# A two-layer trunk: first products of three feed-forwards by seven block products in place of eight

## The chip, the cores and the metric

The kernel runs on one core of a Trainium2 chip. The metric is the device time of one execution in microseconds (us); a median over several executions is given, and the profile shows one execution instruction by instruction. The engines are named as in the profile: PE (TensorE, matrix products; PEld is its loading of weights), DVE (VectorE), ACT (ScalarE), POOL (GpSimd), SP (issues the loads).

## The reference, cut to what matters

```python
def ffn_sublayer(x, mod, k, g, w_in, w_out):
    h = modulated_norm(x, mod, k, g)              # RMS norm, (1 + scale), shift
    gt, up = jnp.split(h @ w_in, 2, axis=-1)      # 1024 -> 2 x 2816
    return x + 0.5 * mod[:, None, 3 * k + 2] * ((jax.nn.silu(gt) * up) @ w_out)
...
def ada_params(cond, w_ada, b_ada):               # shifts, scales and gates of a layer
    m = jax.nn.silu(cond) @ w_ada + b_ada         # 1024 -> 9 x 1024, for two conditions
...
# two layers, each: feed-forward, mixer (attention, pooling, convolution), feed-forward
# 128 context tokens and 512 latent tokens, all float32, 1024 channels
```

## The kernel before

There are six stages, one for each sublayer (l, n): feed-forwards (0,0), (0,2), (1,0) and (1,2), and a mixer (n = 1) in each layer. In the trace they lie at about 20 to 531 us, (0,0); 531 to 779, mixer; 779 to 1268, (0,2); 1268 to 1753, (1,0); 1753 to 1991, mixer; 1991 to 2466, (1,2).

The 640 tokens stay on the chip, channels on the partitions (`xT`, eight tiles of 128 channels), and are worked on in two halves of 320 columns. A float32 product is made of three in a reduced float32 format (`mm3`): weights and inputs are each split into a high and a low part, and high·high, high·low and low·high are summed in PSUM. `split_w` does that for a weight tile: ACT copies the high part (L163), POOL subtracts to give the low part (L164). For an input DVE subtracts (`split`, L149 and L150).

A feed-forward has 22 tiles j of 128 gate columns and 128 up columns. For each tile `up(j)` loads a gate and an up weight tile (128 x 1024, one load of 512 KB each), and multiplies each with the eight channel tiles of both halves: 2 x 2 x 8 x 3 = 96 matmuls of 128x128 by 320 columns. `gated` then takes the SiLU of the gate (ACT, L476), multiplies with up (DVE, L477) and splits the result into `g`. After certain tiles `down(ch)` multiplies a group of finished tiles (`FF_CHUNKS`, here of 6, 6, 6 and 4 tiles) with the second weights and adds the result to the tokens (`update_x`, L407); the last group goes through `last_product`, beside the norm of the next stage.

The modulation (`ada_params`) of later sublayers is computed beside the feed-forwards, in 32 chunks of 512 columns: 14 in (0,0), 11 in (0,2), 7 in (1,0), none in (1,2). A chunk (`ada_vector`) has four loads of 512 KB into `adaw` and, on DVE, two multiplications by a column (L287) and 14 multiply-adds (L289), all of 128x512, into a tile `part`. Later `side` ends it: eight small products on PE sum `part` over its partitions ("the pick", L296), DVE copies the sums (L252), PE transposes them (L253), DVE adds the bias (L254). `spread` says after which tiles a chunk is ended and the next one begun.

Loads, tiles and semaphores are handed out by a framework that also orders each engine's instructions. A tile of a pool with n buffers can be written only when the one handed out n tiles before it has been read for the last time. The pools that matter: `raw` (3 buffers, weights as loaded), `adaw` (2), `wh` and `wl` (4 each, split weights), `part` (1 buffer), `acc` (4 PSUM banks).

## Time and profile before

| | before |
|---|---|
| median of 3 runs (lowest to highest) | 2467.27 us (2467.14 to 2467.51) |
| span of the profiled execution | 2466.6 us |
| PE busy | 2387.6 us, 97% of the span, 16414 matmuls |
| DVE busy | 1346.8 us, 55% |
| ACT busy | 747.1 us, 30% |
| POOL busy | 786.3 us, 32% |
| loads into SBUF and stores | 246.58 MB, 100 GB/s over the span |

The profiled execution's own time is its span, 2466.6 us; it stands 0.7 us below the median of the runs. Shares are means over stages that differ: a feed-forward keeps PE busy nearly throughout, a mixer less. DVE's share differs between feed-forwards by the number of modulation chunks in them.

### The profile page before, as it was taken

How to read it: one execution, taken by the hardware profiler on the slowest of the kernel's cores; microseconds unless marked ns; L12 is line 12 of the kernel's file. 1: busy time of each engine (PE TensorE's matmuls, PEld its weight loads, DVE VectorE, ACT ScalarE, POOL GpSimd, SP SyncE). 2: the span in 40 equal slices, each digit the busy share in tenths (PEclk: the TensorE clock that was granted, in tenths of full speed). 3: DMA queues.
4: the chain of work that ended last, by engine and by line, in shares of the span. 5: the costliest groups of instructions: out<-in, count | busy, mean ns of one | idle time of the engine just before them, and what ended most of it. 6: DMA issues, size and time to landing. Idle time of an engine off the chain costs nothing.

```text
span 2466.6 us, 39767 instructions
## 1 busy us (share of the span) xinstructions
PE 2387.6 (97%) x16414; PEld 2311.5 (94%) x16414; DVE 1346.8 (55%) x2550; ACT 747.1 (30%) x1405; POOL 786.3 (32%) x383
## 2 busy tenths in 40 slices
PE   7999999999898999999999999999998989999999
PEld 6999999989878999999989999999897789999999
DVE  5565747877867464536683435253787662222222
ACT  4322222244455222222142222221454642221221
POOL 2433333333311433233323333333332133333331
PEclk9999999999999999999999999999999999999999
DMA  8444545523201443434423324232221022223221
GB/s 277 119 138 137 162 128 162 175 60 80 53 27 35 118 139 112 137 112 137 146 60 108 107 86 129 78 117 81 68 64 43 18 77 67 80 69 86 77 61 69
DMA packets 357246, 246.58 MB, mean 100 GB/s; under 512 B 25704, under 2 KB 317896, under 8 KB 357064
## 3 DMA queue, kind: packets, MB, share of 16 engines
q1 hardware_dynamic: 356884, 243.97, 33.3%
q8 instruction: 129, 2.11, 0.4%
q14 instruction: 53, 0.43, 0.1%
q10 hardware_dynamic: 180, 0.07, 0.0%
HBM read 241.12 MB, written 2.88 MB: 99 GB/s over the span
## 4 chain that ended last, share of the span: by engine, by line
PE 82%; DVE 12%; issue 2%; DMA 2%; ACT 2%; POOL 0%; ACTq 0%; DVEq 0%; SPq 0%; POOLq 0%
PE acc L329 26%; PE acc L330 25%; PE acc L331 25%; DVE part L289 3%; DVE tmp L378 1%; PE po L930 1%; DMA adaw<-in_w_ada 1%; PE acc L890 1%; PE mis L941 1%; DVE ssq L240 1%; DVE g L150 1%; DVE qw L762 1%; DVE x L407 1%; DVE t L341 1%; DVE h L394 1%
## 5 line engine op out<-in xcount | busy, mean ns | idle before, releaser
L164 POOL TENSOR_TENSOR wl<-raw,wh 128x1024 fp32r<-128x1024 f32 (+1 forms) x330 | 757.5, 2296 | 1568.5 <-ACT wh L163 1472.2
L329 PE MATMUL acc<-h,wh 128*128 128x320 f32 (+1 forms) x3264 | 1022.4, 314 | 14.9 <-ACT h L393 9.2
L330 PE MATMUL acc<-h,wh 128*128 128x320 f32 (+1 forms) x3264 | 1019.6, 313 | 14.0 <-DVE h L394 10.1
L331 PE MATMUL acc<-h,wl 128*128 128x320 f32 (+1 forms) x3264 | 1013.5, 311 | 0.0
L329 PEld LDWEIGHTS acc<-h,wh 128*128 128x128 f32 x3264 | 619.3, 190 | 25.5 <-ACT h L393 11.2
L330 PEld LDWEIGHTS acc<-h,wh 128*128 128x128 f32 x3264 | 619.7, 190 | 19.1 <-DVE h L394 12.5
L163 ACT ACTIVATE wh<-raw 128x1024 fp32r<-128x1024 f32 (+1 forms) x332 | 330.7, 996 | 1008.1 <-PE acc L330 507.7
L331 PEld LDWEIGHTS acc<-h,wl 128*128 128x128 f32 x3264 | 620.6, 190 | 0.2 <-issue 0.2
L330 PE MATMUL acc<-g,wh 128*128 128x320 f32 x1408 | 437.0, 310 | 0.0
L329 PE MATMUL acc<-g,wh 128*128 128x320 f32 x1408 | 435.9, 310 | 0.0
L331 PE MATMUL acc<-g,wl 128*128 128x320 f32 x1408 | 434.6, 309 | 0.0
L289 DVE SCALAR_TENSOR_TENSOR part<-adaw,c,part 128x512 f32<-128x512 f32 x448 | 363.0, 871 | 28.6 <-DMA adaw<-in_w_ada 28.6
L477 DVE TENSOR_TENSOR sg<-acc,sg 128x320 f32<-128x320 f32 x132 | 61.1, 488 | 498.8 <-PE acc L331 496.9
L407 DVE SCALAR_TENSOR_TENSOR x<-acc,gate,x 128x128 f32<-128x128 f32 (+2 forms) x384 | 155.4, 434 | 305.7 <-PE acc L331 305.4
L329 PEld LDWEIGHTS acc<-g,wh 128*128 128x128 f32 x1408 | 264.4, 188 | 1.6 <-issue 1.4
L331 PEld LDWEIGHTS acc<-g,wl 128*128 128x128 f32 x1408 | 265.3, 188 | 0.2
L330 PEld LDWEIGHTS acc<-g,wh 128*128 128x128 f32 x1408 | 264.3, 188 | 0.3
L150 DVE TENSOR_TENSOR g<-sg,g 128x320 fp32r<-128x320 f32 x176 | 187.4, 1100 | 31.6 <-ACT g L149 29.8
L476 ACT ACTIVATE sg<-acc 128x320 f32<-128x320 f32 x132 | 56.9, 431 | 300.6 <-PE acc L331 289.8
L329 PE MATMUL acc<-mix,wh 128*128 128x320 f32 x256 | 83.2, 325 | 13.2 <-DVE u L856 12.7
L149 ACT ACTIVATE g<-sg 128x320 fp32r<-128x320 f32 x176 | 75.5, 462 | 45.1 <-DVE sg L477 25.9
L331 PE MATMUL acc<-mix,wl 128*128 128x320 f32 x256 | 82.5, 322 | 0.0
(170 smaller groups left out, 1591.9 us busy)
## 6 DMA issues: line engine op xcount, KB each, us to landing
raw<-in_w_ffn_in SPq DMA_DIRECT2D x176, 512.0 KB
adaw<-in_w_ada SPq DMA_DIRECT2D x144, 512.0 KB
raw<-in_w_ffn_out SPq DMA_DIRECT2D x96, 384.0 KB
raw<-in_w_in SPq DMA_DIRECT2D x20, 512.0 KB
raw<-in_w_ffn_out SPq DMA_DIRECT2D x16, 512.0 KB
raw<-in_w_in SPq DMA_DIRECT2D x16, 256.0 KB
raw<-in_w_out SPq DMA_DIRECT2D x8, 512.0 KB
raw<-in_w_out SPq DMA_DIRECT2D x16, 256.0 KB
```

The source lines that it names most:

```text
L149: nc.scalar.activation(h, src, AF.Copy)
L150: nc.vector.tensor_tensor(lo, src, f32(h), op=ALU.subtract)
L163: nc.scalar.activation(h, raw, AF.Copy)
L164: eng.tensor_tensor(lo, raw, f32(h), op=ALU.subtract)
L240: nc.vector.tensor_tensor(ssq[:, c:e], ssq[:, c:e], sq[:, : e - c], op=ALU.add)
L289: nc.vector.scalar_tensor_tensor(part[:, j, :], r[:, k, :], c, part[:, j, :], op0=ALU.mult, op1=ALU.add)
L329: nc.tensor.matmul(out, wh, xh, start=start, stop=False)
L330: nc.tensor.matmul(out, wh, xl, start=False, stop=False)
L331: return nc.tensor.matmul(out, wl, xh, start=False, stop=stop)
L407: nc.vector.scalar_tensor_tensor(xT[t][:, s:e], ps[:, s - a : e - a], gates[l][n][:, t, j : j + 1], xT[t][:, s:e], op0=ALU.mult, op1=ALU.add,)
L476: nc.scalar.activation(sg, gate[:, :HALF], AF.Silu)
L477: nc.vector.tensor_tensor(sg, up[:, :HALF], sg, op=ALU.mult)
```

## The change: what it does

In the feed-forwards (0,2), (1,0) and (1,2) the tiles j = 3 to 21 are computed by seven block products in place of eight: 19 tiles in each, 57 in all. (0,0) and tiles 0 to 2 stay as they are. A block is half of the channels (four channel tiles) by half of the tokens, for up or for gate. Plainly a tile needs 2 x 2 x 2 = 8 such products of 4 x 3 = 12 matmuls; now there are seven, 84 matmuls, over sums of weight blocks and of input blocks.

- The input sums are made once in a stage (`seven`).
- The weight sums are made for each tile (`fast_weights`): four additions of 128x512 on DVE give two tiles of sums, `one` and `two`, in a new pool `sums` of two buffers. The low parts of both are made on DVE (128x1024 each), those of the up tile (128x1024) and of a quarter of the gate tile (`late`, 128x512) on POOL. ACT makes three high parts of 128x1024 and one of 128x512, in place of two of 128x1024.
- The results are put together from PSUM: ACT copies three of 128x320 out (`kept`), DVE adds three to them (`added`). Products 3 and 4 and the gating of tile j (`fast_ends`) come after product 1 of tile j + 1; `a` and `c` are `acc` banks, `b` is a bank of the mixer's pool `one_p`.

To make room: `raw` (now 4 buffers) serves weights and modulation loads alike, `part` of a modulation chunk is now one of the two `sums` tiles, several small tiles share nine `tmp` buffers, and the mixers load their tables each time. `FF_CHUNKS` has five groups (5, 5, 4, 4, 4), those of four with two column tiles to a load.

The comments were taken out of the file, so line numbers differ.

```diff
-FF_CHUNKS = ((0, 6), (6, 12), (12, 18), (18, 22))
+FF_CHUNKS = ((0, 5), (5, 10), (10, 14), (14, 18), (18, 22))
+PLAIN = 3
...
-    rawp = pool("raw", 3)
-    adaw = pool("adaw", 2)
+    rawp = pool("raw", 4)
...
+    sump = pool("sums", 2)
...
     def split_w(raw, nk, width, eng=nc.gpsimd):
...
-        part = small.tile([P, 2, 512], F32, name="part", bufs=1)
+        part = sum_tile().rearrange("p (j c) -> p j c", j=2)
         for q in range(4):
-            r = load_ada(l, ci, q, adaw.tile([P, 2, 512], F32, tag="adaw", name="adaw"))
+            r = load_ada(l, ci, q, raw_tile().rearrange("p (k c) -> p k c", k=2))
...
+        def fast_weights(j):
+            nk = KD // 2
+            up, *_ = load_raw(w_in, DFF + j * P)
+            gate, *_ = load_raw(w_in, j * P)
+            a1, a2, d1, d2 = up[:, :nk, :], up[:, nk:, :], gate[:, :nk, :], gate[:, nk:, :]
...
+            one, two = view(sum_tile()), view(sum_tile())
+            ups = split_w(up, KD, P)
+            add(one[:, :nk, :], a1, d1)
+            add(one[:, nk:, :], d1, d2)
+            add(two[:, :nk, :], one[:, nk:, :], a1)
+            add(two[:, nk:, :], two[:, :nk, :], a2)
+            late = split_w(d2, nk, P)
+            twos = split_w(two, KD, P, nc.vector)
+            ones = split_w(one, KD, P, nc.vector)
...
+            return {1: first(ups), 2: second(ups), 3: second(twos), 4: late, 5: second(ones), 6: first(twos), 7: first(ones)}
+
+        def fast_product(ps, w, x, start):
+            wh, wl = w[x]
+            for p in range(4):
+                mm3(ps[:, :HALF], wh[:, p, :], wl[:, p, :], *hs.operand(x, p), start and p == 0, p == 3, not start)
...
+        def fast_ends(j, w, a, c, up1, gate1, gate2):
+            fast_product(a, w, 3, False)
+            fast_product(c, w, 4, False)
+            gs[j] = slot(F32R, name="g")
+            nc.scalar.activation(gate2, gate2, AF.Silu, scale=-1.0)
+            nc.vector.tensor_tensor(gate2, a[:, :HALF], gate2, op=ALU.mult)
+            split(gs[j][:, 0, HALF:T], gs[j][:, 1, HALF:T], gate2)
+            added(gate1, c)
+            nc.scalar.activation(gate1, gate1, AF.Silu, scale=-1.0)
+            nc.vector.tensor_tensor(gate1, up1, gate1, op=ALU.mult)
+            split(gs[j][:, 0, 0:HALF], gs[j][:, 1, 0:HALF], gate1)
+
+        def fast_ups(j, ends):
+            w = fast_weights(j)
+            a, c = acc(), acc()
+            b = one_p.tile([P, 512], F32, tag="po", name="po")
+            fast_product(a, w, 1, True)
+            up1 = kept(a)
+            ends()
+            fast_product(a, w, 6, False)
+            gate1 = kept(a)
+            fast_product(b, w, 2, True)
+            added(up1, b)
+            fast_product(c, w, 7, True)
+            fast_product(a, w, 5, False)
+            gate2 = kept(a)
+            added(gate2, c)
+            return lambda: fast_ends(j, w, a, c, up1, gate1, gate2)
...
         for j in range(2, NJ):
-            up(j)
+            if first or j < PLAIN:
+                up(j)
+            else:
+                ends = fast_ups(j, ends)
             side(j)
```

How the order on PE stands now is shown at the end of a modulation chunk in (0,2). In the names, `mis` is the PSUM bank of a pick, `sums_9563` the chunk's `part`, `wh_9606` and `wl_9607` the parts of `two` of the tile that has just begun, `wh_9610` those of its `one`; the first row is the end of that tile's product 2.

```order
L338 MATMUL po_9616<-h_7919,wl_9595 128x320
L303 MATMUL mis_9719<-sums_9563,pick_176 32x128 [waits DVE_49]
L303 MATMUL mis_9719<-sums_9563,pick_176 32x128 x3
L260 MATMUL mis_9719<-ident_85,arow_9728 128x128 [waits DVE_49]
L336 MATMUL acc_9614<-h_7963,wh_9606 128x320 [waits Activation_49]
L337 MATMUL acc_9614<-h_7963,wh_9606 128x320
L336 MATMUL acc_9615<-h_7963,wh_9610 128x320 [waits Activation_49]
L337 MATMUL acc_9615<-h_7963,wh_9610 128x320
L338 MATMUL acc_9614<-h_7963,wl_9607 128x320 [waits DVE_49]
```

The pick now stands between product 2 of a tile and its products 6 and 7, which read the split sums `two` and `one`; the same pattern stands at each of the 18 picks in (0,2) and (1,0).

At the same place DVE has this order (`sums_9592` is `one`, `sums_9593` is `two`, `raw_9588` the up tile, `arow` the pick's sums).

```order
L659 TENSOR_TENSOR part_9629<-po_9616,part_9629 128x320 [waits PE_49]
L156 TENSOR_TENSOR g_9655<-part_9521,g_9655 128x320 [waits Activation_49]
L630 TENSOR_TENSOR sums_9593<-sums_9592,raw_9588 128x512 [waits PE_49]
L259 COPY arow_9728<-mis_9719 128x128
L630 TENSOR_TENSOR sums_9593<-sums_9593,raw_9588 128x512 [waits DVE_49]
L261 TENSOR_TENSOR mods1_181<-mis_9719,cols72_2418 128x8 [waits PE_49]
L322 SCALAR_TENSOR_TENSOR gain10_9430<-mods1_181,cols120_119 128x8 [waits DVE_49]
L171 TENSOR_TENSOR wl_9607<-sums_9593,wh_9606 128x1024 [waits Activation_49]
L171 TENSOR_TENSOR wl_9611<-sums_9592,wh_9610 128x1024 [waits Activation_49]
```

With two buffers in `sums`, `two` is written into the one that held the chunk's `part`: its first addition waits for PE, that is for the pick. Before the change a pick stood on PE like this, in (0,2) too (`acc_8672` is the end of one tile, `acc_8751` and `acc_8752` the start of the next).

```order
L331 MATMUL acc_8672<-h_7891,wl_8668 128x320
L296 MATMUL mis_8732<-part_8584,pick_176 32x128 x8
L329 MATMUL acc_8751<-h_7835,wh_8747 128x320 [waits Activation_49]
L330 MATMUL acc_8751<-h_7835,wh_8747 128x320
L331 MATMUL acc_8751<-h_7835,wl_8748 128x320 [waits Pool_49]
L329 MATMUL acc_8752<-h_7835,wh_8747 128x320 [waits Activation_49]
L253 MATMUL mis_8732<-ident_85,arow_8741 128x128 [waits DVE_49]
```

There the products behind the pick waited for ACT and POOL, not for anything that the pick had to release.

## Rows read from the trace of the kernel before

**Rows 1.** The page: busy time by engine, and the chain that ended last.
```profile
PE 2387.6 (97%) x16414; PEld 2311.5 (94%) x16414; DVE 1346.8 (55%) x2550; ACT 747.1 (30%) x1405; POOL 786.3 (32%) x383
...
PE 82%; DVE 12%; issue 2%; DMA 2%; ACT 2%; POOL 0%; ACTq 0%; DVEq 0%; SPq 0%; POOLq 0%
```
**Rows 2.** Windows by stage: length; PE, PEld, DVE, ACT, POOL; PEclk; DMA; GB/s.
```profile
779.00:1268.00 489.00, 482.25 (x3360) 474.58 (x3360) 274.88 (x453) 122.79 (x204) 164.07 (x72) 0.99 0.40 119
1268.00:1753.00 485.00, 478.14 (x3293) 472.76 (x3294) 229.31 (x368) 122.61 (x204) 165.68 (x81) 0.99 0.33 96
1991.00:2466.00 475.00, 470.44 (x3196) 469.27 (x3195) 134.19 (x220) 108.69 (x178) 150.03 (x68) 0.99 0.25 73
```
**Rows 3.** Timeline of PE in (1,2); 183 matmuls from first row to second.
```profile
2119.80 0.31 PE L331 MATMUL acc<-g,wl 128*128 128x320 f32 x1
...
2146.64 0.31 PE L331 MATMUL acc<-g,wl 128*128 128x320 f32 x1
```
**Rows 4.** Timeline of ACT in (0,2), first SiLU of three tiles in turn.
```profile
844.93 0.44 ACT L476 ACTIVATE sg<-acc 128x320 f32<-128x320 f32 x1 [5.64 <-PE acc L331]
...
859.02 0.44 ACT L476 ACTIVATE sg<-acc 128x320 f32<-128x320 f32 x1 [3.73 <-PE acc L331]
...
873.99 0.44 ACT L476 ACTIVATE sg<-acc 128x320 f32<-128x320 f32 x1 [5.58 <-PE acc L331]
```
**Rows 5.** Four views by line: shortest, median and longest duration in ns.
```profile
L164 DVE TENSOR_TENSOR wl<-raw,wh x2: 1218/1222/1225, 28.8 to 29.9; 128x1024 fp32r<-128x1024 f32 x2
...
L759 DVE TENSOR_TENSOR rope<-rope,sinT x10: 679/1090/1198, 603.0 to 1863.0; 128x512 f32<-128x512 f32 x10
...
L287 DVE TENSOR_SCALAR part<-adaw,c x64: 469/476/2661, 66.8 to 1642.7; 128x512 f32<-128x512 f32 x64
...
L150 DVE TENSOR_TENSOR g<-sg,g x44: 476/1184/2446, 2005.4 to 2389.2; 128x320 fp32r<-128x320 f32 x44
```
**Rows 6.** Groups by line and shape, whole span: busy, mean ns, idle before.
```profile
L477 DVE TENSOR_TENSOR sg<-acc,sg 128x320 f32<-128x320 f32 x132 | 61.1, 488 | 498.8 <-PE acc L331 496.9 <-ACT sg L476 1.8
...
L252 DVE COPY arow<-mis 128x128 f32<-128x128 f32 x36 | 10.3, 286 | 12.8 <-PE mis L268 9.8 <-PE mis L296 2.4
...
L164 POOL TENSOR_TENSOR wl<-raw,wh 128x1024 fp32r<-128x1024 f32 x234 | 573.4, 2451 | 1149.0 <-ACT wh L163 1057.8 <-PE acc L330 37.0 <-PE acc L331 28.2
...
L760 POOL TENSOR_TENSOR rope<-qw,cosT 128x512 f32<-128x512 f32 x8 | 10.4, 1298 | 47.1 <-DVE qw L748 33.6 <-PE acc L331 13.5
...
L163 ACT ACTIVATE wh<-raw 128x1024 fp32r<-128x1024 f32 x236 | 249.6, 1058 | 627.2 <-issue 315.4 <-PE acc L330 298.3 <-POOL wl L164 13.2
```
**Rows 7.** Timeline of DVE in (0,0), three tiles with a chunk to each.
```profile
261.06 2.67 DVE L150 TENSOR_TENSOR g<-sg,g 128x320 fp32r<-128x320 f32 x2
...
264.60 4.05 DVE L289 SCALAR_TENSOR_TENSOR part<-adaw,c,part 128x512 f32<-128x512 f32 x6
...
269.63 5.91 DVE L289 SCALAR_TENSOR_TENSOR part<-adaw,c,part 128x512 f32<-128x512 f32 x8 [0.91 <-DMA adaw<-in_w_ada]
...
276.97 1.15 DVE L150 TENSOR_TENSOR g<-sg,g 128x320 fp32r<-128x320 f32 x2
...
284.09 6.97 DVE L289 SCALAR_TENSOR_TENSOR part<-adaw,c,part 128x512 f32<-128x512 f32 x8 [0.41 <-DMA adaw<-in_w_ada]
...
292.48 1.59 DVE L150 TENSOR_TENSOR g<-sg,g 128x320 fp32r<-128x320 f32 x2
```
**Rows 8.** Windows, sum over the three tiles of 253.26 to 299.70 us.
```profile
sum 46.44, PE 45.80 PEld 43.99 DVE 38.05 ACT 11.25 POOL 14.35; mean PE 15.27 PEld 14.66 DVE 12.68 ACT 3.75 POOL 4.78
```
**Rows 9.** Windows around the end of (0,2), columns as in rows 2.
```profile
1260.00:1262.00 2.00, 0.03 (x1) 0.00 (x0) 2.00 (x1) 0.10 (x1) 1.87 (x1) 1.00 0.12 36
1262.00:1264.00 2.00, 0.89 (x2) 0.59 (x3) 1.99 (x7) 1.41 (x3) 0.00 (x0) 0.71 0.48 138
1264.00:1272.00 8.00, 5.92 (x20) 5.12 (x20) 7.36 (x17) 3.55 (x9) 2.44 (x1) 0.50 0.33 98
```
**Rows 10.** Waits of PE's weight loads: us in total, times, longest.
```profile
PEld mis L296 <- DVE part L289: 12.0, 21, 1.2
```

More of the change, by code (lines that the diff above doesn't have):

```diff
@@ L140, in raw_tile, with sum_tile @@
         return rawp.tile([P, 1024], F32, tag="raw", name="raw")
+    def sum_tile(name="sums"):
+        return sump.tile([P, 1024], F32, tag="sums", name=name)
     def load_ada(l, ci, q, tile):
@@ L374, in norm_tail @@
             if hf == 0:
-                hs.append(slot(F32R, name="h", shape=(2, T if shifted else T + 2)))
-            tmp = small.tile([P, HALF], F32, tag="tmp", name="tmp", bufs=3)
+                hs.tiles.append(slot(F32R, name="h", shape=(2, T if shifted else T + 2)))
+            tmp = small.tile([P, HALF], F32, tag="tmp", bufs=TMPS, name="tmp")
             for s, e, j in SEGS[hf]:
@@ L387, in norm_tail @@
                 eng = nc.gpsimd if hf else nc.vector
-                high = nc.scalar.activation(hs[t][:, 0, a:b], tmp, AF.Copy)
-                last = eng.tensor_tensor(hs[t][:, 1, a:b], tmp, f32(hs[t][:, 0, a:b]), op=ALU.subtract)
+                high = nc.scalar.activation(hs.tiles[t][:, 0, a:b], tmp, AF.Copy)
+                last = eng.tensor_tensor(hs.tiles[t][:, 1, a:b], tmp, f32(hs.tiles[t][:, 0, a:b]), op=ALU.subtract)
                 continue
@@ L402, in norm_tail, with __init__, part, operand @@
         return None if shifted else (high, last)
+    class Plain:
+        def __init__(self):
+            self.tiles = []
+            self.order = range(KD)
+        def part(self, k, hf, extra=0):
+            a, b = HALVES[hf]
+            return self.tiles[k][:, 0, a : b + extra], self.tiles[k][:, 1, a : b + extra]
+    class Seven:
+        def __init__(self):
+            self.order = [k for p in range(4) for k in (p, p + 4)]
+            self.b1c1, self.b2, self.c2, self.first, self.second = [], [], [], [], []
+        def part(self, k, hf, extra=0):
+            if hf == 0:
+                t = self.b1c1[k % 4][:, k // 4]
+            else:
+                t = (self.c2 if k >= 4 else self.b2)[k % 4 // 2][:, k % 2]
+            return t[:, 0, :], t[:, 1, :]
+        def operand(self, x, p):
+            if x == 1:
+                return self.part(p, 0)
+            if x == 2:
+                return self.part(p + 4, 0)
+            if x == 3:
+                return self.part(p + 4, 1)
+            t = {5: self.first[p][:, 0], 4: self.first[p][:, 1], 6: self.second[p][:, 0], 7: self.second[p][:, 1]}[x]
+            return t[:, 0, :], t[:, 1, :]
@@ L457, in part @@
                 b += 2
-            for k in range(KD):
-                mm3(
-                    ps[:, : b - a],
-                    w[0][:, k, :],
-                    w[1][:, k, :],
-                    hs[k][:, 0, a:b],
-                    hs[k][:, 1, a:b],
-                    k == 0,
-                    k == KD - 1,
-                )
+            for x, k in enumerate(hs.order):
+                high, low = hs.part(k, hf, b - HALVES[hf][1])
+                mm3(ps[:, : b - a], w[0][:, k, :], w[1][:, k, :], high, low, x == 0, x == KD - 1)
                 yield
@@ L516, in down @@
             nj = j1 - j0
[L517 to L531 removed]
+            wide = 2 if nj <= 4 else 1
@@ new lines, in fast_product, with temp, kept, added @@
+        def fast_product(ps, w, x, start):
+            wh, wl = w[x]
+            for p in range(4):
+                mm3(ps[:, :HALF], wh[:, p, :], wl[:, p, :], *hs.operand(x, p), start and p == 0, p == 3, not start)
+        def temp():
+            return small.tile([P, HALF], F32, tag="tmp", bufs=TMPS, name="part")
+        def kept(ps):
+            t = temp()
+            nc.scalar.activation(t, ps[:, :HALF], AF.Copy)
+            return t
+        def added(t, ps):
+            nc.vector.tensor_tensor(t, ps[:, :HALF], t, op=ALU.add)
@@ L533, in ffn @@
         ch = 0
+        ends = lambda: None
         if first:
@@ L539, in ffn @@
         for j in range(2, NJ):
-            up(j)
+            if first or j < PLAIN:
+                up(j)
+            else:
+                ends = fast_ups(j, ends)
             side(j)
-            if ch < 2 and j == FF_CHUNKS[ch][1] + 1:
+            if ch < len(FF_CHUNKS) - 2 and j == FF_CHUNKS[ch][1] + (2 if first else 1):
                 down(ch)
                 ch += 1
-        down(2)
-        j0, j1 = FF_CHUNKS[3]
+        ends()
+        down(ch)
+        j0, j1 = FF_CHUNKS[-1]
         ws = [load_cols(w_out[j0 * P : j1 * P, :], m * 256, 256) for m in range(4)]
@@ L1167, in trunk_kernel @@
         last = x == len(steps) - 1
-        new = []
+        fast = not last and steps[x + 1][1] != 1
+        new = Seven() if fast else Plain()
         if last:
@@ L1177, in nxt @@
                 heads.append(norm_head(hf))
-                if hf == 1:
+                if hf == 1 and fast:
+                    seven(*steps[x + 1], new, heads)
+                elif hf == 1:
                     for h in range(2):
```

161 lines of the change are left out of this document (101 added, 60 removed).

## The prediction

> **What bounds the kernel now.** I read the page first. PE is busy for 97% of the span and carries 82% of the chain that ended last [rows 1]; DVE is next on the chain with 12% but is busy for only 55%. So PE sets the time, and a matmul taken away is worth its place in the row unless another engine then ends later. Such means hide where that may happen, so the windows by stage come next [rows 2]: DVE works 275 us of 489 in (0,2), 229 of 485 in (1,0) and 134 of 475 in (1,2). The difference is the modulation: 11, 7 and 0 chunks. PE is at full clock (0.99) in all three. The price of a matmul is read from the timeline: 183 of them start within 26.84 us [rows 3], so one takes 0.1467 us, a plain tile of 96 takes 14.08 and a fast one of 84 takes 12.32. In (0,2) the first SiLU comes at 844.93, 859.02 and 873.99 [rows 4]: 14.09 us for one tile, 29.06 for two with a chunk between them, 0.90 over two bare ones. Before, then, a chunk costs PE the pick alone, and its DVE work is hidden: PE waits for the sums at 21 picks, for 12.0 us in all [rows 10].
>
> **What is removed.** 57 tiles lose 12 matmuls each: 684 x 0.1467 = 100.3 us, 33.4 in each of the three stages. This is certain; whether PE can use it is not.
>
> **What is added, on DVE.** Prices: an addition of 128x512 from two SBUF inputs 0.68 us, the shortest of a line with this shape; a low part of 128x1024 1.22; a 128x320 operation 0.48 (0.476 as the shortest from SBUF, 0.488 with PSUM) [rows 5, 6]. A fast tile has four additions (2.7), two low parts (2.4) and seven operations of 320 columns (three sums, two products, two low parts: 3.4): 8.5 us, where a plain one has four (1.9). A chunk has two multiplications at 0.476 [rows 5] and 14 multiply-adds at 0.675 (4.05 for 6, [rows 7]): 10.4 us. So two tiles with a chunk ask 2 x 8.5 + 10.4 + 0.3 for the pick's copy = 27.7 us of DVE, while PE has only 24.64 + 0.90 = 25.54 us of work. DVE is the longer of the two before any wait is counted.
>
> Three things come on top.
> - **POOL in DVE's way.** The rows show that DVE's operations with two SBUF inputs lengthen beside POOL's subtraction: in (1,2) the low part L150 has a median of 1184 ns and a least of 476 [rows 5]. Two a tile give 1.4 us lost against 4.9 us of POOL (two of 2.45, [rows 6]), 0.29 of POOL's time. In (0,0), where DVE is busy for 38.05 of 46.44 us [rows 8], eight multiply-adds took 5.91 and 6.97 us where 5.40 is due, and pairs of L150 2.67, 1.15 and 1.59 where 0.95 is due [rows 7]: 4.6 us lost in three tiles with 14.35 us of POOL [rows 8], a share of 0.32. In the changed kernel POOL has 2.45 + 1.30 a tile [rows 6], 7.5 a pair. At 0.32 that is 2.4 us; the bounds are 0 and 7.5. I take the share of (0,0), whose DVE is the nearest to a full one.
> - **Waits for ACT and PE** between dependent steps of DVE: the high part of `two` is 1.06 us of ACT [rows 6], and each gating has a SiLU and a high part between DVE's steps; the order puts multiply-adds of the chunk in most of those gaps. I estimate 2.0 us a pair, between 1 and 3.
> - **The pick.** `two` takes the buffer that the chunk's `part` had, so it is made after the pick, and PE needs it for its very next product. While PE stands, this runs in a row: addition 0.68, the pick's copy 0.29, addition 0.68, high part 1.06, low part 1.22, together 3.9 and with handovers about 4.3 us. It costs DVE nothing more, but PE's own path is then 25.54 + 4.3 = 29.8 us, already over the 29.06 of before. So a pair with a chunk can hardly gain, even with a DVE that is never held.
>
> DVE's sum is 27.7 + 2.4 + 2.0 = 32.1 us a pair, bounds 29.8 and 37.2 (POOL in full). The loss against 25.54 is 6.6.
>
> The Trainium skill, in "SBUF — State Buffer", section "SBUF: two separate sides", says that the second SBUF input of DVE and POOL's reads share a port that is locked for a whole instruction by whichever starts first, so that the other waits in full. The L150 of 1184 to 2446 ns bears the lock out. By that rule a DVE that always has such work waiting would lose all of POOL's time; the third rival gives it its time.
>
> **The sum, against the profiled span of 2466.6 us.**
> - Removed matmuls: -100.3.
> - Of the 18 chunks beside fast tiles, 13 end clear of a `down` (8 in (0,2), 5 in (1,0)): 13 x 6.6 = +85.5.
> - The other five end beside a `down`, whose matmuls (some 28 to 35 us) hide DVE's work but not the chain behind the pick: I take 3.5 each, +17.5, bounds 0 and 21.
> - Clock: at the end of (0,2) PE stood through 1260 to 1262, and the granted clock was then 0.71 and for 8 us 0.50 [rows 9]. A stand of 4.3 us at each pick is of that size. A drop of 8 us costs 4 us of PE, of which a pair held by DVE has 2.3 to spare; I take 0.7 for each of 18, +13, bounds 0 and 45.
> - Tiles without a chunk: 8.5 of DVE, 1 to 2 of waits and 1.2 to 3.75 of POOL make 10.7 to 14.3 against PE's 12.32. I take the lower half, and a slight loss of +3 in all.
> - Heads of the three stages: input sums and their low parts, some 14 us of DVE, behind the norm while PE has tiles 0 to 2: +4, bounds 0 and 15.
> - (0,0): a tile takes 46.44 / 3 = 15.48 us [rows 8] against 14.08 + 0.90, and DVE waits 0.91 and 0.41 for the chunk's loads [rows 7]. Four shared buffers may give a part of that back, or may put a weight load behind the four loads of a chunk: -3, bounds -5 and +28.
> - The fifth `down` group: the matmuls of the second product stay the same in number, and 16 more sets of L407 in each of four stages lie under PE-bound `down` products, where DVE is mostly idle: 0. Without that cover one would cost about half a microsecond.
>
> Together -100.3 + 85.5 + 17.5 + 13 + 3 + 4 - 3 = +19.7: a span of 2486.3. The median of the runs lies 0.7 above the profiled span, so I predict **2487 us**. By stage, (1,2) falls by some 30 us to about 445, (1,0) stays within some 10 of its 485, and (0,2) grows by 20 to 40.
>
> **The rivals.** The sign hangs on one number: with the other terms as they are, the change breaks even at a loss of 65.8 / 13 = 5.1 us, a pair of 30.6 us.
> - *DVE keeps up, only the pick's chain counts.* POOL is held by DVE rather than the other way round, and a pair takes PE's 29.8: 13 x 4.3 = 55 in place of 85.5, no clock term, no +3: 2487 - 30 - 13 - 3 = 2441, with a chain of 3.5 and cheaper `down` places 2423; range 2420 to 2462. For it: DVE's own 27.7 lies below 29.8, and in (0,0) a chunk in each tile cost PE only 0.5 us. Against it: what DVE lost beside POOL there.
> - *Everything is hidden.* Also the chain behind the pick lies beside other products: 2467 - 100 + 4 - 3, about 2368. The order speaks against it, since the products queued behind the pick on PE read `two`.
> - *POOL holds DVE in full.* A pair takes 37.2: 13 x 5.1 = +66 more, and tiles without a chunk go over 12.32 by about 1 us, some 20 more: about 2573. For it: L150 met POOL nearly every time in (1,2), though DVE had little else to do. Against it: 0.32 in (0,0).
> - *Loads in the shared buffers hold PE in (0,0).* 14 chunks by 2 us: +28 and the 3 given up, about 2518. Against it: DVE's waits for loads there are 0.91 and 0.41 us with two buffers for a chunk [rows 7], and four shared ones hold as much in flight.
> - That the change does not do what it says is excluded by the order: 84 matmuls stand in a fast tile.
>
> **How the numbers follow.** Chances: my forecast 0.45, with a range of its own of 2465 to 2535; DVE keeps up 0.29; everything hidden 0.05; POOL in full 0.14; loads in (0,0) 0.07. Differences under 0.2% (4.9 us) are about what a measurement of this kernel cannot tell from no change. Of the forecast's 0.45 some 0.06 lies within that, the rest above; of the second case 0.26 is faster and 0.03 the same. So faster 0.31, same 0.09, slower 0.60. The range 2420 to 2560 leaves out the hidden case (0.05), the upper half of POOL in full (0.07) and a few hundredths of the second.
>
> **What would show it.** In (1,2) the starts of product 1 in successive tiles should be 12.3 to 12.6 us apart. In (0,2), two tiles with a chunk should take about 32, with DVE busy without a gap, and PE should stand about 4 us behind the pick, waiting for the low part of `two`; DVE's 1024-wide low parts should have a median well over 1.22 where POOL runs. I am wrong if pairs take under 30.6, if the clock drops to half at most picks (then 2520 or more), or if (0,0) changes by more than 10 us.

## The result

The changed kernel takes 2573.77 us (median of four runs, 2571.76 to 2583.31) against 2467.2 (2467.14 to 2467.51): a ratio of 1.0438, 95% interval 1.042 to 1.0455. It is slower, as forecast, but by 106.6 us where 20 was forecast, and outside the range of 2420 to 2560. The profiled execution is the longest of the four; its span is 2581.5 us, 7.7 above the median, so it is compared with the span of 2466.6 before.

The page of the changed kernel, busy time and chain:

```profile
PE 2351.1 (91%) x15730; PEld 2250.5 (87%) x15730; DVE 1832.0 (71%) x3195; ACT 952.6 (37%) x1750; POOL 750.0 (29%) x383
...
PE 58%; DVE 28%; ACT 5%; issue 4%; DMA 4%; POOL 0%; SPq 0%; ACTq 0%; DVEq 0%; POOLq 0%
```

The 684 matmuls are gone (16414 to 15730), PE's share of the chain that ended last has fallen from 82% to 58% [rows 1], and DVE's has risen from 12% to 28%. Where the time went is read from the windows by stage, cut here at the norm's last product between two stages (columns as in rows 2); the six stages in order:

```profile
0.00:556.90 556.90, 510.47 (x3716) 494.61 (x3716) 368.95 (x633) 147.60 (x253) 182.91 (x99) 0.98 0.46 143
556.90:800.70 243.80, 226.62 (x1436) 202.40 (x1436) 185.01 (x448) 127.17 (x293) 64.60 (x34) 0.95 0.20 53
800.70:1356.40 555.70, 482.14 (x3131) 462.17 (x3131) 426.96 (x659) 189.37 (x315) 153.47 (x72) 0.94 0.35 105
1356.40:1886.90 530.50, 467.06 (x3048) 452.93 (x3048) 381.41 (x578) 185.41 (x308) 150.82 (x79) 0.95 0.31 94
1886.90:2130.20 243.30, 226.03 (x1437) 201.89 (x1437) 185.08 (x448) 127.28 (x293) 64.17 (x33) 0.96 0.19 53
2130.20:2581.50 451.30, 438.74 (x2965) 436.46 (x2965) 284.63 (x432) 175.73 (x288) 134.07 (x68) 0.99 0.25 75
```

Against 489, 485 and 475 us [rows 2], (0,2) is 67 longer, (1,0) 46 longer and (1,2) 24 shorter; (0,0) is 16 longer than its 540.5 before, and the mixers 5 each. Only (1,2), which has no chunks, keeps what the matmuls give, and PE's granted clock is 0.94 and 0.95 of full speed in the other two, where it was 0.99. The timeline of ACT shows the tiles: each row is the first SiLU behind the sums of a tile (L666), in (0,2) and then in (1,2).

```profile
899.46 0.47 ACT L666 ACTIVATE part<-part 128x320 f32<-128x320 f32 x1 [0.96 <-DVE part L659]
...
971.46 0.47 ACT L666 ACTIVATE part<-part 128x320 f32<-128x320 f32 x1 [1.15 <-DVE part L659]
985.50 0.47 ACT L666 ACTIVATE part<-part 128x320 f32<-128x320 f32 x1 [2.47 <-DVE part L659]
1006.14 0.47 ACT L666 ACTIVATE part<-part 128x320 f32<-128x320 f32 x1 [1.23 <-DVE part L659]
...
2186.59 0.47 ACT L666 ACTIVATE part<-part 128x320 f32<-128x320 f32 x1 [0.47 <-DVE part L659]
2198.90 0.47 ACT L666 ACTIVATE part<-part 128x320 f32<-128x320 f32 x1 [0.47 <-DVE part L659]
2211.21 0.47 ACT L666 ACTIVATE part<-part 128x320 f32<-128x320 f32 x1 [0.47 <-DVE part L659]
...
2272.92 0.47 ACT L666 ACTIVATE part<-part 128x320 f32<-128x320 f32 x1 [0.47 <-DVE part L659]
```

A tile of (1,2) takes 12.31 us, as forecast. Two tiles with a chunk in (0,2), 971.46 to 1006.14, take 34.68 (three other such pairs 34.8 to 35.0), where 29.06 was before [rows 4] and 32.1 was forecast. The window of that pair (columns as in rows 2):

```profile
971.46:1006.14 34.68, 28.58 (x187) 26.81 (x186) 32.21 (x46) 13.15 (x23) 8.14 (x4) 0.90 0.40 122
```

The timelines of PE and DVE at the pick just before this pair, with PE's stands at the pick inside it as the last two rows of PE:

```profile
956.14 0.64 PE L303 MATMUL mis<-sums,pick 128*32 128x128 f32 x16
958.57 0.33 PE L260 MATMUL mis<-ident,arow 128*128 128x128 f32 x1 [1.78 <-DVE arow L259]
960.32 0.41 PE L336 MATMUL acc<-h,wh 128*128 128x320 f32 x1 [1.42 <-ACT wh L170]
...
961.27 0.53 PE L336 MATMUL acc<-h,wh 128*128 128x320 f32 x1 [0.39 <-ACT wh L170]
...
992.37 0.47 PE L260 MATMUL mis<-ident,arow 128*128 128x128 f32 x1 [2.49 <-DVE arow L259]
994.98 0.64 PE L336 MATMUL acc<-h,wh 128*128 128x320 f32 x1 [2.14 <-ACT wh L170]
```

```profile
957.63 0.68 DVE L630 TENSOR_TENSOR sums<-sums,raw 128x512 f32<-128x512 f32 x1
958.23 0.28 DVE L259 COPY arow<-mis 128x128 f32<-128x128 f32 x1
958.43 0.68 DVE L630 TENSOR_TENSOR sums<-sums,raw 128x512 f32<-128x512 f32 x1
...
960.30 2.36 DVE L171 TENSOR_TENSOR wl<-sums,wh 128x1024 fp32r<-128x1024 f32 x2 [0.91 <-ACT wh L170]
```

The chain behind the pick is there as read from the order: addition, copy, addition, high part, low part, and PE waits 1.78 + 1.42 + 0.39 = 3.6 us for it, and 2.49 + 2.14 = 4.6 us at the next pick. It waits for the copy and for the high parts, not for the low part that the prediction named. The windows of 2 us over the first of the two places (columns as in rows 2) show the granted clock after it, 0.85, then 0.50, which is the lower of its two levels (1.2 and 2.4 GHz), then 0.80:

```profile
958.00:960.00 2.00, 0.33 (x1) 0.14 (x1) 1.35 (x5) 0.79 (x1) 0.00 (x0) 1.00 0.00 0
960.00:962.00 2.00, 1.29 (x5) 1.03 (x6) 1.70 (x2) 2.00 (x3) 0.00 (x0) 0.85 0.83 249
962.00:964.00 2.00, 2.00 (x10) 2.00 (x8) 2.00 (x2) 0.16 (x1) 1.76 (x1) 0.50 0.04 13
964.00:966.00 2.00, 2.00 (x13) 2.00 (x12) 2.00 (x2) 0.44 (x1) 0.88 (x1) 0.80 0.00 0
```

Summed over such windows as busy time times the missing share of the clock, (0,2) loses 28.3 us and (1,0) 22.1 to the clock, 3.7 and 4.6 before. And the waits of PE's weight loads over the whole span (us in total, times, longest); the last row is the kernel before:

```profile
PEld mis L260 <- DVE arow L259: 60.8, 26, 5.2
PEld acc L336 <- ACT wh L170: 56.4, 43, 4.2
PEld mis L359 <- DVE ssq L247: 24.6, 8, 8.7
...
PEld mis L253 <- DVE arow L252: 0.9, 2, 0.7
```

The wait for the copy behind a pick was 0.9 us in all before and is now 60.8: 24.0 in (0,2), 19.6 in (1,0) and 17.3 in (0,0). The wait ahead of a pick, 12.0 us before [rows 10], has all but gone (0.4). In the third line 8.7 and 8.6 us are a stand before each mixer, 2.5 each before, that was not in the forecast.

### The profile page after: what moved, and what is told of

It is laid out like the page before. It is cut to its first block, busy times and chain, and to the rows that moved or that the text cites. A ratio compares the mean times of both kernels' runs of the same rounds, so it can differ in the third digit from the quotient of the medians.

```text
span 2581.5 us, 39442 instructions
## 1 busy us (share of the span) xinstructions
PE 2351.1 (91%) x15730; PEld 2250.5 (87%) x15730; DVE 1832.0 (71%) x3195; ACT 952.6 (37%) x1750; POOL 750.0 (29%) x383
## 3 DMA queue, kind: packets, MB, share of 16 engines
q1 hardware_dynamic: 340932, 244.88, 31.5%
## 4 chain that ended last, share of the span: by engine, by line
PE 58%; DVE 28%; ACT 5%; issue 4%; DMA 4%; POOL 0%; SPq 0%; ACTq 0%; DVEq 0%; POOLq 0%
PE acc L336 18%; PE acc L337 17%; PE acc L338 17%; DVE sums L296 10%; DVE sums L630 4%; ACT wh L170 2%; DMA raw<-in_w_ffn_in 2%; DVE ssq L247 2%; DVE g L156 2%; PE po L1084 1%; DMA raw<-in_w_ada 1%; DVE x L502 1%; PE acc L1044 1%; PE mis L1095 1%; DVE wl L171 1%
## 5 line engine op out<-in xcount | busy, mean ns | idle before, releaser
L171 POOL TENSOR_TENSOR wl<-raw,wh 128x1024 fp32r<-128x1024 f32 (+2 forms) x330 | 720.8, 2190 | 1721.7 <-ACT wh L170 1645.7
L336 PE MATMUL acc<-h,wh 128*128 128x320 f32 (+1 forms) x2808 | 900.0, 323 | 77.2 <-ACT wh L170 34.0
L337 PE MATMUL acc<-h,wh 128*128 128x320 f32 (+1 forms) x2808 | 889.8, 318 | 6.8 <-DVE h L396 3.9
L338 PE MATMUL acc<-h,wl 128*128 128x320 f32 (+1 forms) x2808 | 884.3, 317 | 9.3 <-POOL wl L171 9.3
L336 PEld LDWEIGHTS acc<-h,wh 128*128 128x128 f32 x2808 | 546.6, 195 | 105.2 <-ACT wh L170 44.5
L337 PEld LDWEIGHTS acc<-h,wh 128*128 128x128 f32 x2808 | 547.8, 195 | 9.8 <-DVE h L396 4.1
L170 ACT ACTIVATE wh<-raw 128x1024 fp32r<-128x1024 f32 (+2 forms) x332 | 305.6, 922 | 601.1 <-PE acc L337 349.5
L296 DVE SCALAR_TENSOR_TENSOR sums<-raw,c,sums 128x512 f32<-128x512 f32 x448 | 412.7, 973 | 5.4 <-DMA raw<-in_w_ada 5.4
L502 DVE SCALAR_TENSOR_TENSOR x<-acc,gate,x 128x128 f32<-128x128 f32 (+2 forms) x480 | 193.8, 434 | 275.2 <-PE acc L338 274.1
L336 PEld LDWEIGHTS acc<-g,wh 128*128 128x128 f32 x1408 | 267.8, 190 | 32.5 <-issue 17.4
L171 DVE TENSOR_TENSOR wl<-sums,wh 128x1024 fp32r<-128x1024 f32 x114 | 136.9, 1223 | 54.9 <-ACT wh L170 54.8
L170 ACT ACTIVATE wh<-sums 128x1024 fp32r<-128x1024 f32 x114 | 117.2, 1053 | 139.8 <-PE acc L337 63.1
L156 DVE TENSOR_TENSOR g<-part,g 128x320 fp32r<-128x320 f32 x114 | 115.3, 1012 | 38.4 <-ACT g L155 35.0
L630 DVE TENSOR_TENSOR sums<-raw 128x512 f32<-128x512 f32 x114 | 115.5, 1050 | 13.4 <-DMA raw<-in_w_ffn_in 12.8
```

The lines of the kernel that those rows point to most:

```text
L156: nc.vector.tensor_tensor(lo, src, f32(h), op=ALU.subtract)
L170: nc.scalar.activation(h, raw, AF.Copy)
L171: eng.tensor_tensor(lo, raw, f32(h), op=ALU.subtract)
L296: nc.vector.scalar_tensor_tensor(part[:, j, :], r[:, k, :], c, part[:, j, :], op0=ALU.mult, op1=ALU.add)
L336: nc.tensor.matmul(out, wh, xh, start=start, stop=False, skip_group_check=onto)
L337: nc.tensor.matmul(out, wh, xl, start=False, stop=False, skip_group_check=onto)
```

## The experiments

Spans of stages below are cut at the same product of the norm, from one execution each; before has 540.5, 239.2, 488.2, 484.3, 238.3 and, to the span's end, 476.1 us.

**1. The chunk's sums in their own buffer** (e_part).

```diff
-TMPS = 9
+TMPS = 8
...
-        part = sum_tile().rearrange("p (j c) -> p j c", j=2)
+        part = small.tile([P, 2, 512], F32, name="part", bufs=1)
```

> The chunk's sums get a buffer of their own again (one of the nine small tmp buffers is given up for the room), so that the pick no longer stands ahead of the weight sums. If the chain behind the pick with the clock drops that follow it is the cost (18 stands of PE of 3.2 to 5 us, and 45 us of clock), PE's stands at picks vanish, the clock in (0,2) stays near 0.99 and the time falls by 60 to 90 us, to about 2490 to 2510. If DVE's own work beside POOL bounds the pairs, two tiles with a chunk stay at 33 us or more (DVE busy 32.2 of 34.7 us now) and the time falls by 30 us or less, to 2545 or more; PE's waits then only move to other products.

2653.77 us, 80 slower than changed, which is neither of the two expected figures. The stages say why: (0,0) took 700.6 us in place of 556.9, while (0,2) fell to 530.0 and (1,0) to 486.1, 26 and 44 less. The chain was a cost, and something else made (0,0) stand.

**2. Loads shared, nothing else** (b_raw), on the kernel before.

```diff
-    rawp = pool("raw", 3)
-    adaw = pool("adaw", 2)
+    rawp = pool("raw", 4)
...
-            r = load_ada(l, ci, q, adaw.tile([P, 2, 512], F32, tag="adaw", name="adaw"))
+            r = load_ada(l, ci, q, raw_tile().rearrange("p (k c) -> p k c", k=2))
```

> The kernel before with one pool of 4 buffers for weights and modulation loads in place of 3 and 2; the sums stay in their own buffer, nothing else changes. If the shared loads are what made (0,0) with the change to the mixer 21 us longer, this kernel is slower than before by 10 to 25 us, with the loss in (0,0). If the loss in (0,0) came from the second buffer for the chunk's sums (which lets DVE run ahead of the copy of a pick) or from the five down groups, this is within 5 us of before.

2656.44 us against 2468.5, 188 slower, far more than either guess: (0,0) took 701.8 us, (0,2) 519.2, some 30 more than before, and (1,0) 483, as before. The timelines of PE, DVE and ACT at one pick in (0,0):

```profile
170.41 0.33 PE L252 MATMUL mis<-ident,arow 128*128 128x128 f32 x1 [1.11 <-DVE arow L251]
177.92 0.63 PE L328 MATMUL acc<-g,wh 128*128 128x320 f32 x1 [7.18 <-ACT wh L162]
183.11 0.64 PE L330 MATMUL acc<-g,wl 128*128 128x320 f32 x1 [4.29 <-POOL wl L163]
```

```profile
172.04 9.36 DVE L288 SCALAR_TENSOR_TENSOR part<-raw,c,part 128x512 f32<-128x512 f32 x14
```

```profile
177.03 0.84 ACT L162 ACTIVATE wh<-raw 128x768 fp32r<-128x768 f32 x1 [6.36 <-DMA raw<-in_w_ffn_out]
```

The next chunk cannot begin before the pick has freed the one `part`; its four loads fill the shared buffers until then, and the weights behind them in the rotation come after the chunk, so PE stands for 11 to 12 us, at 11 places in (0,0) and at two in (0,2). The changed kernel's two buffers for the sums hide this (in e_part, with one, (0,0) is as long as here): they are what makes the shared loads bearable, and they are also what puts the chain behind the pick.

**3. Both right: own buffer only beside (0,2) and (1,0)** (e_split).

```diff
-        part = sum_tile().rearrange("p (j c) -> p j c", j=2)
+        if l == 0:
+            part = sum_tile().rearrange("p (j c) -> p j c", j=2)
+        else:
+            part = small.tile([P, 2, 512], F32, name="part", bufs=1)
```

(With one tmp buffer less, as in the first.)

> As changed, but the chunks beside (0,2) and (1,0) have a buffer of their own for their sums, while those beside (0,0) keep the pair of buffers (one tmp buffer is given up for the room). (0,0) should be as changed, 561 us to the mixer's start and not 705. If the pick's chain is worth what the stages of the run with one buffer throughout showed, (0,2) takes 535 and (1,0) 490 us and the time falls by some 70 us, to about 2505; both stages are still longer than the 489 and 484 of before, which is what is left to DVE and POOL. If the low 490 of (1,0) hung on (0,0), the gain is under 40 us.

2500.04 us, 73.7 less than changed, as expected; (0,2) 527.2, (1,0) 487.0. Of the single edits to the changed kernel this one returns most. It is a net figure: the chunks of (0,2) now have one buffer beside shared loads, the state of run 2, which with plain tiles cost this stage some 30 us. A pair with a chunk (970.19 to 1001.68, window row as in rows 2):

```profile
970.19:1001.68 31.49, 27.68 (x181) 25.99 (x182) 31.11 (x45) 12.90 (x22) 8.63 (x4) 0.95 0.46 135
```

DVE is busy for 31.11 of 31.49 us: without the chain DVE sets the pair, near the 32.1 of the forecast (three other such pairs took 31.7 to 32.5).

**4. A quarter of the chunk's work** (e_few), and the same on the split buffers, beside (0,2) and (1,0) only (e_split_few).

```diff
-            for k in range(2):
+            for k in range(2 if q == 0 else 0):
```

> Each chunk does 4 of its 16 multiplications (the other three quarters of the modulation's sums are left out; all loads stay). DVE loses 8.1 us a chunk, the pick and the chain behind it stay. If DVE's work is the bound, two tiles with a chunk fall from 34.7 us to what PE with the chain and the half clock needs, about 30 to 31, and the time falls by some 18 x 4 = 70 us or more, (0,0) included. If the chain is the whole cost, the pairs stay within 1 us of 34.7 and the time falls by less than 25 us.

> As the run with the split buffers, and the chunks beside (0,2) and (1,0) do 4 of their 16 multiplications (the rest of these sums is left out, all loads stay). Neither the chain nor a long chunk is left. If these two with POOL's share are all that keeps the 33 us a stage from showing, (0,2) falls to 475 us or less and (1,0) to 465 or less, and pairs of tiles with a chunk to 27 us or less. If something else holds tiles with a chunk (loads in the shared buffers, the order on DVE), (0,2) stays over 490.

Both leave three quarters of the sums of those chunks out, so they are tests and not kernels to use. e_few: 2515.45 us, 58 less, with (0,0) at 533.4 and the pairs of (0,2) at 31.7: less than DVE's theory asked and more than the chain's, since the chain stayed. DVE is busy for 24.1 us of such a pair, so PE's path with the chain sets it. e_split_few: 2433.26 us, ratio 0.986 to before; (0,2) 478.9, (1,0) 468.5, a little above the expected bounds. Two tiles with a chunk:

```profile
1046.74:1072.25 25.51, 25.51 (x187) 25.11 (x186) 21.72 (x33) 13.16 (x23) 8.13 (x4) 1.00 0.54 164
```

PE is busy throughout, at full clock, in 25.51 us: the forecast's sum of PE's own work, 25.54. With neither chain nor long chunk PE is the bound again, in three of the five pairs of (0,2) that are clear of a `down` (25.5 to 26.4 us). The other two took 31.1 and 29.5: PE stood 4.3 and 2.4 us behind the pick there, while DVE waited 4.6 and 2.7 us for a weight load before it came to the copy.

**5. POOL reads nothing in fast tiles** (e_noread); the low parts of the up and late weights are zeros.

```diff
+        if low:
+            eng.tensor_tensor(lo, raw, f32(h), op=ALU.subtract)
+        else:
+            nc.gpsimd.memset(f32(lo), 0.0)
```

> In fast tiles POOL fills the low parts of the up and late weights with zeros instead of subtracting (those low parts are left out), so POOL reads nothing there and each fill is shorter. If POOL's reads hold DVE up, the multiply-adds and additions go back to 0.68 us each, two tiles with a chunk fall by 4 to 6 us (34.7 to about 30), and the time falls by 40 to 80 us. If POOL matters only through PE waiting for its low parts (about 1 us a pair), the time falls by 15 us or less.

2512.15 us, 62 less. A pair:

```profile
950.90:981.64 30.74, 27.72 (x187) 26.72 (x186) 26.30 (x46) 13.34 (x22) 2.90 (x4) 0.94 0.47 138
```

DVE is busy for 26.30 us, 32.21 in the changed kernel's pair of 34.68: POOL's reads cost DVE 5.9 us in a pair with 8.14 us of POOL, a share of 0.73. The pair is then PE's own path with the chain (29.8 in the forecast, here 30.7). The two figures are near each other in part by luck: PE stood 3.0 us where 4.3 was priced, and worked 27.7 where 25.5 was, as its clock was 0.94.

**6. Five down groups** on the kernel before (b_chunks), and four again in (0,0) of the changed kernel (e_c4).

```diff
-FF_CHUNKS = ((0, 6), (6, 12), (12, 18), (18, 22))
+FF_CHUNKS = ((0, 5), (5, 10), (10, 14), (14, 18), (18, 22))
...
-            if ch < 2 and j == FF_CHUNKS[ch][1] + 1:
+            if ch < len(FF_CHUNKS) - 2 and j == FF_CHUNKS[ch][1] + (2 if first else 1):
```

(The groups of four come with two column tiles to a load, and in (0,0) a `down` comes one tile later, both as in the changed kernel; e_c4 takes both back in (0,0).)

> The kernel before with five down groups (5, 5, 4, 4, 4) in place of four, nothing else. My sum had them at nothing: within 5 us of before. If they are what lengthens the stand at the norm after a feed-forward (8.4 us for the sum of squares in the changed kernel against 2.1 to 2.6), this is slower by 10 to 25 us, with the loss at the ends of the stages.

> As changed, but (0,0) keeps the four down groups of before; the shared loads and the chunk's pair of buffers stay. The kernel before with five groups lost 13.5 us in (0,0); the changed kernel lost 16.4 there. If the groups are the cause, (0,0) comes back to 543 us or less and the time falls by 10 to 16 us, to about 2560. If it is the shared loads, (0,0) stays over 553.

b_chunks: 2492.98 us, ratio 1.0097 (1.0082 to 1.0112): 24.6 us from the groups alone, 13.5 in (0,0) and 10 in (0,2), the stages with most chunks, none in (1,0) or (1,2). PE waits there at picks for sums that are not ready (3.1, 2.9 and 4.2 us at three of them, 1.2 at most before [rows 10]) and for L407 (1.2); the stands before the mixers did not come. e_c4: 2565.2 us, 8.6 less; (0,0) 545.0. How much of the changed kernel's (0,0) this is, one execution does not tell well: its 556.9 came out at 548.6 in run 5 and 547.0 in run 7, whose (0,0) is the same program, so by the stages the groups are 2 to 4 us there.

**7. PE kept at work in the stand** (e_fill).

```diff
+        if l == 1:
+            for _ in range(12):
+                nc.tensor.matmul(ps[:, 256:512], fill_w, fill_x, start=True, stop=True)
```

> As changed, with 12 matmuls of 128x256 that compute nothing behind each pick beside (0,2) and (1,0), so that PE works for some 1.4 us of its stand. All waits stay. If the half clock after the stands is a cost of its own, it is granted less often or for a shorter time (42 us of clock were lost in the two stages over before), and the time falls by 15 to 40 us. If DVE sets the pace of those tiles anyway, PE at half clock costs nothing there: the clock may rise, the time stays within 8 us.

2567.22 us, 6.6 less, with the mean clock 0.970 in place of 0.961 and 15 us less lost to the clock in (0,2) and (1,0). So of the part that was given back, over half was no cost of its own: where DVE is late anyway, PE may be slow. The other 27 of the 42 us lost over before stayed lost in this run, so what they cost is not shown.

**8. Seven products in (1,2) alone** (e_last_best), with the loads, the chunk's buffer and the groups of before; in (1,2) itself the five groups stay, and the weight sums lie in the two buffers of the modulation loads.

```diff
-        fast = not last and steps[x + 1][1] != 1
+        fast = not last and x + 1 == len(steps) - 1
```

> Seven products in (1,2) alone, with the loads, the chunk's sums and the down groups of the other stages as in the kernel before (in (1,2), which has no chunks, the weight sums lie in the two buffers of the modulation loads). By the stages of the changed kernel (1,2) falls from 476 to 456 us and all else stays: about 2447, faster than both. If the seven products cost something outside their stage, 2460 or more.

2463.58 us, ratio 0.9981 (0.9972 to 0.9991), 17 short of the expectation: (1,2) fell to 456.6 us, but 13 us went in the other stages and in the norms between them, with single stands of 8.4 and 10 us for the sum of squares.

**9. The norm's small tiles in buffers of their own** on that (e_last_tags), and on the changed kernel (e_tags).

```diff
-            sq = small.tile([P, HALF], F32, tag="tmp", bufs=TMPS, name="sq")
+            sq = small.tile([P, HALF], F32, tag="square", name="sq")
...
-            tmp = small.tile([P, HALF], F32, tag="tmp", bufs=TMPS, name="tmp")
+            tmp = small.tile([P, HALF], F32, tag="tmp", bufs=3, name="tmp")
```

(`r0` and `t1` with two buffers each in the same way; the fast tiles' three sums use the same four groups.)

> Seven products in (1,2) alone, as in the run with the loads and groups of before, and in addition the small tiles of the norm are again in buffers of their own (nine in four groups, as before) and not in one ring of nine. That run lost 3 to 5 us in each mixer stage and 2 to 4 in (0,2) and (1,0), with one stand of 8.4 us for the sum of squares where before had 2.1 and a few short ones. If the ring is the cause, this falls from 2463.6 to about 2450; if the tables loaded in each mixer or the 22 slots are, it stays within 4 us of 2463.6.

> As changed, but the small tiles of the norm are in buffers of their own again (nine in four groups) in place of one ring of nine; everything else stays, chain, groups and seven products in three stages. In the kernel with seven products in (1,2) alone this gave 17.6 us. If the ring costs the same here, the time falls to about 2556, with the single stand of 8.4 us before the mixers gone and the mixer stages back from 243 to 239 us. If the stages with seven products hide it or need the ring, it stays within 5 us of 2573.8.

e_last_tags: **2445.94 us, ratio 0.9908 (0.9893 to 0.9923)**: the fastest kernel of the study that computes everything, 0.9% under before and clear of the noise. Its stages (columns as in rows 2; both mixers left out) are those of before in the first five, within 2.5 us:

```profile
0.00:539.60 539.60, 510.52 (x3731) 494.60 (x3732) 331.39 (x627) 150.86 (x262) 178.59 (x101) 0.98 0.49 147
...
776.50:1263.90 487.40, 480.51 (x3360) 473.00 (x3360) 288.44 (x469) 123.52 (x205) 165.76 (x72) 0.99 0.43 124
1263.90:1746.80 482.90, 476.32 (x3291) 471.09 (x3291) 226.48 (x366) 122.50 (x205) 167.07 (x80) 0.99 0.33 97
...
1985.20:2442.30 457.10, 438.89 (x2965) 435.88 (x2965) 288.35 (x432) 176.13 (x288) 136.59 (x68) 0.99 0.25 76
```

e_tags: 2564.08 us, 9.7 less than changed, the mixer stages back to 238 us and the stands before them to 2.8 and 2.5. One ring of nine buffers hands out tiles in turn, so a short-lived tile can be made to wait for a long-lived one; with the same nine in four groups the stands are gone. Which tile waited for which was not traced.

**10. The three repairs together** (e_all: 3, 9 and the groups of 6, with one buffer fewer for the split late weights), and the same without seven products in (0,2) (e_all_two).

> Seven products in the three stages, with the three repairs together: the chunks beside (0,2) and (1,0) with a buffer of their own, four down groups in (0,0), the norm's small tiles in their own buffers (the room comes from one instead of two buffers for the split late weights). One by one they gave 73.7, 8.6 and 9.7 us. If they add up, this takes about 2482, and what is left over before is DVE's work in tiles with a chunk, two of which stay at 31 to 32 us; (0,2) stays over 510. If the single gains overlap, 2495 or more.

> The same with seven products in (1,0) and (1,2) alone; (0,2), with 11 chunks, is plain again. If DVE's work beside the chunks bounds, (1,0), with 7 chunks, comes out at 475 to 485 us against 484 of before, (0,2) at 488, and the time is 2440 to 2450. If seven products gain in (1,0) once the chain is gone, as its tiles without a chunk suggest, it is under 2440, the fastest of all.

e_all: 2495.61 us, ratio 1.0115; the single gains do not add up (92 singly, 78 together), and (1,0) came out at 498.4 where e_split had 487.0; whether the late weights' single buffer or the small tiles' groups did that was not tried. e_all_two: 2487.81 us; (0,2), plain again, took 519.0 in place of 488.2. The picture of run 2 is back there, as the chunk has one buffer and the loads are shared: PE stands 7.6 and 4.0 us in turn at each of two places. (1,0) took 498.1, as in e_all and over the 475 to 485 of the expectation; with the loads shared, this run does not tell what seven products in (1,0) are worth by themselves.

## Why the prediction was wrong

**The direction held, and part of the mechanism.** Tiles of (1,2), which has no chunks, gain in full: PE's busy time there fell by 32 us, where 228 matmuls weigh 33.4, and the tiles run at 12.31 us; the stage as a whole kept 24 of the 30 forecast, as PE stands at its head (2.4 us) and at three `down` products (1.6, 1.6 and 2.5). Tiles with a chunk lose because DVE has more to do than PE. Both paths that I priced for a pair exist, each by itself: DVE's at 31.5 us once the chain is gone (e_split; 32.1 forecast), PE's with the chain at 30.7 once POOL leaves DVE alone (e_noread; 29.8 forecast), and PE's own at 25.5 with neither chain nor long chunk (e_split_few; 25.5 forecast).

**The steps that failed** are two. The first is the sentence on the pick, "It costs DVE nothing more", and the sum's treating a pair as the longer of the two paths. The chain is DVE's and PE's turn by turn: while PE stands, DVE waits for the pick and for ACT's high part (0.91 us above), and once PE resumes it is late for what DVE adds next. The pair took 34.7, 3.2 over DVE's own 31.5, and in (1,0), where DVE has slack (381 us busy of 530), the chain cost as much or more: e_split took 28.5 us from (0,2) and 43.5 from (1,0). For the chain my sum had 17.5 at the `down` places and 13 of clock, 30.5 in all; undoing it gave 73.7.

The second is the term for the five chunks that end beside a `down`, whose matmuls were to "hide DVE's work but not the chain behind the pick", at 3.5 us each. Two tiles with a `down` of 240 matmuls and a chunk took 72.00 us in (0,2) (899.46 to 971.46 above); two with the same `down` and no chunk took 61.71 in (1,2) (2211.21 to 2272.92). Less the 0.90 of a pick that is 9.4 us more. The other four such places had 10.2, 7.7, 9.8 and 9.5 more than their like in (1,2): 46.6 in all, where the sum had 17.5 and its upper bound was 21. The chain's stands there were 3.2 to 3.6 us, as priced. But the `down` products themselves stood, 17.8 us over the five, for the update of the tokens (L502), which comes behind the chunk's work on DVE; the longest such stand, with the multiply-adds ahead of it:

```profile
1681.48 7.25 DVE L296 SCALAR_TENSOR_TENSOR sums<-raw,c,sums 128x512 f32<-128x512 f32 x5
...
1689.86 0.61 PE L336 MATMUL acc<-g,wh 128*128 128x320 f32 x1 [5.26 <-DVE x L502]
```

With the chain gone (e_split) the first of the five places still took 71.1 us, with one stand of 8.0 for this update. So a `down` does not hide DVE's work; it waits for it.

**Terms that were mis-sized.**
- POOL in DVE's way: 2.4 us a pair from a share of 0.32, measured 5.9 (0.73). DVE's own work was put too high, 27.7 against 26.3, and so were its waits, 2.0 against 0.4 in e_split's pair. That 32.1 came so near that pair's 31.5 is luck: 27.7 + 2.4 + 2.0 stood for some 26.3 + 4.8 + 0.4, and the errors cancelled.
- The five groups: 0 in the sum, with DVE "mostly idle" as the cover. On the kernel before they cost 24.6, in (0,0) of the changed one 8.6 by the runs' medians. The cover was looked for under the new L407 alone; the long waits in b_chunks are at picks, whose place between tiles and `down` products had moved.
- Heads: 4 for the input sums. The stands before the mixers came from the ring of small tiles, which I had not priced: 9.7.
- Clock: 13, with 45 as the bound; some 42 us were lost in the two stages, but giving 15 of them back returned only 6.6 of the time, so by that run the term was not the miss.

By stage, the sum's own terms make +40 in (0,2), +14 in (1,0), -31 in (1,2) and -3 in (0,0); the profiled execution has +67, +46, -25 and +16, and +10 in the two mixers. So some 60 of the 95 us by which its span lies over the forecast's 2486.3 are in the two stages with chunks, and 26 to 29 of these at the five `down` places (with the clock's 0.7 for each or without). How the rest divides between the chain, POOL and the half clock cannot be added up from the runs: undoing the chain, POOL's reads or most of the chunk's work alone gave 73.7, 61.6 and 58.3 us (the last with (0,0) in it), and each of the three shortens the same pairs.

Of the prediction's own signs of being wrong two came: the clock fell to half behind the pick that is shown, with a time over 2520, and (0,0) grew by more than 10 us in the profiled execution (by 6.5 in run 7). One sign of its being right did not: DVE's 1024-wide low parts kept their median (1.22 us); the additions, the multiply-adds and the 320-wide low parts met POOL in their place.

**The rivals.** My third rival had POOL holding DVE in full. Its 2573 is the measured time, but by another way: it had pairs of 37.2 and slower tiles in (1,2), and neither came. The loads in shared buffers did not hold (0,0) in the changed kernel by themselves, but only because `part` had two buffers: with one, they cost 188 us, far beyond the 28 of that rival. The order spoke against everything being hidden, and rightly.

## What to carry to other kernels

When a change gives one engine's saved time to a second engine as work, price the second engine stage by stage, and where the two meet in a chain of turns (a pick, a copy, an addition, a split), add the chain to the longer path and do not take the larger of the two (here it came to 3.2 us a pair on DVE's 31.5). Nor does a long product hide the second engine's work if it needs a small update from that engine itself. A buffer shared between a load that is held for long and loads that are needed soon couples them: look at who frees the tile that comes just before in the rotation. And a saving that holds in the stage without side work may be kept by making the change there alone: seven products in (1,2), with the other stages' buffers untouched, won 22 us where three stages lost 107.
